# A hybrid attention and recurrence block: sticks times values in plain float32, and four more merge gates in the second stage

## The chip, the cores and the metric

The kernel runs on one core of a Trainium2 chip. The metric is the device time of one execution in microseconds (us); lower is better. PE is the matmul engine (PEld its weight loads), DVE the vector engine, ACT the scalar engine, POOL the general engine, SP the queue that issues most loads. SBUF is the working memory, PSUM the accumulator memory that PE writes to.

## The reference, cut to what matters

A residual block on 1040 rows (16 learned rows ahead of 1024) of width 1024. One projection makes ten streams. Four of them feed stick-breaking attention with 8 heads of 64 channels, four a gated recurrence (HGRN2), and the last two are sigmoid gates, `gate_sb` and `gate_hg`, with which the two branches are merged channel by channel.

```python
proj = u @ w_in[l]
(sb_q, sb_k, sb_v, sb_gate, hg_q, hg_f, hg_i, hg_gate, gate_sb, gate_hg) = jnp.split(proj, bounds, axis=-1)
...
z = jnp.einsum('bhtd,bhsd->bhts', qb, k)
valid = s_idx[None, :] < t_idx[:, None]
log_beta = jax.nn.log_sigmoid(z)
log_1mb = jnp.where(valid, jax.nn.log_sigmoid(-z), 0.0)
later = lax.cumsum(log_1mb, axis=3, reverse=True) - log_1mb
weights = jnp.where(valid, jnp.exp(log_beta + later), 0.0)
return jnp.einsum('bhts,bhsd->bhtd', weights, v)
...
y_sb = (_stick_breaking(sb_q, sb_k, sb_v) * jax.nn.silu(sb_gate)).astype(dtype)
merged = (jax.nn.sigmoid(gate_sb) * (y_sb @ w_sb_out[l]) + jax.nn.sigmoid(gate_hg) * (y_hg @ w_hg_out[l]))
h = h + merged @ w_out[l]
```

The kernel doesn't form the weights themselves. It keeps the running product of `1 - beta` along the keys (the sticks that are left, called sticks here) and multiplies it by differences of neighbouring values, which gives the same sum.

## The kernel before, in words

Channels lie on the partitions and time along the free axis, in tiles of 128 x 128 where blocks are turned. Precision is kept by splitting: a float32 operand is copied to a reduced float32 type (`F32R`, the high part, on ACT) and the rest is subtracted (the low part, on DVE or POOL). A product is then three matmuls, high x high, high x low, low x high (`piece_quanta`, L244 to L263, matmul L259).

**Stages.** First the input is normalised, turned and split (to 68 us). The second stage (L424 to L500, 67.7 to about 267 us) makes those projections that need no order: queries, attention gates, recurrence queries and gates, and six of the sixteen merge-gate groups (`N_GS`, L40). A *twin* there is 256 output channels for all 1024 rows, computed by a scheme of seven products in place of eight (`product`, L458): each product is 12 matmuls of 512 columns (L466). Its weights are split on ACT (L454) and POOL (L455), sums of them are made on DVE (L448 to L451), and the results go to DRAM through the ACT queue. A merge-gate group that is not made there is made later by `gate_group` (L998): 128 channels, two pieces of 512 rows, 24 matmuls each on L259.

**Attention.** A pair of heads has its key and value projections in `pair_groups` (L526). The differences of values are turned to rows by keys (`v_blocks`, L557; `v_meta_block` for the 16 learned rows) and split in two parts side by side, 64 columns of high and 64 of low part for each head. A unit (`Unit`, L593) is one head and two blocks of 128 queries, g = 0 to 3. `scores` makes the scores (L626), sigmoids on ACT (L628) and the running products on DVE (scans, L631 and L635). `values` turns the sticks in banks of two key blocks (`bank_t`, transposes L668), splits each bank into a high part (ACT, L670) and a low part (DVE, L671), and multiplies (`bank_av`, L682): the values are the stationary operand, and the sticks stream past, 256 queries at a time, four matmuls for a bank, one more for the learned rows (L685). Blocks beyond the diagonal are zeros that were set once. The result has the high values' product on partitions 0 to 63 and the low ones' on 64 to 127; ACT copies one half (L688), DVE adds the other (L689) and applies the last difference and the gate (L693), in the layout that the next stage wants.

**Order.** The program is written out in quanta with a cost in ns each. `zip_quanta` lays the scores of the next unit between the values of the current one, and `interleave` (L297) puts *fill* between the quanta of the main work, in proportion to the costs, 4000 ns ahead (`LEAD_A`). Fill of attention is the next pair's key and value projections, the first recurrence head's projection, and merge-gate groups by `FILL` = (2, 1, 1, 1) for the four pairs (L42, L1093 to L1101). Five more groups are fill of the recurrence (L1128). Buffers of one tag rotate; the tag `wt` has two, which the sticks' banks hold in the attention stage and which the recurrence's queries take after it (L774, loaded through SP at L776). PSUM has two banks for turning (`tr`) and one for this accumulator (`av`).

Of the kernel before, what the change touches and what calls it, by code (L numbers as in the profile page):

```python
# [15 lines left out]
P = 128  # L16
# [20 lines left out]
REAL = [(NM, 512), (NM + 512, 512)]  # L37
FULL = [(0, 348), (348, 346), (694, 346)]
QUART = [(0, 256), (256, 256), (512, 256), (768, 272)]
N_GS = 6  # L40
WS = 456
FILL = (2, 1, 1, 1)  # L42


@with_exitstack
def block_kernel(ctx: ExitStack, tc: tile.TileContext, x, meta, norm_g, w_in, w_sb_out,
# [18 lines left out]
    def sb(tag, shape, dt=F32):  # L65
        p = base if tag in HOME else here[-1]
        return p.tile(shape, dt, tag=tag, name=nm(tag), bufs=BUFS.get(tag, 1))
# [358 lines left out]
    twins += [(C_HQ + 2 * P * k, 2 * k, out_silu(kept_hq, HG_SCALE)) for k in range(2)]  # L426
    twins += [(C_HG + 2 * P * k, 2 * k, out_silu(kept_hg, 1.0)) for k in range(2)]
    twins += [(C_GS + 2 * P * k, 2 * k, out_gate(C_GS)) for k in range(N_GS // 2)]

    def ured(c0, t0):  # L430
        return uh[:, c0:c0 + 4, t0:t0 + HT], ul[:, c0:c0 + 4, t0:t0 + HT]
# [73 lines left out]
    here.append(ctx.enter_context(phase("rest")))  # L505


    t = sb("wt", [P, 2, 2, 512], F32R)
    V.memset(t[:, :, :, 0:P].bitcast(F32), 0.0)
    wt_last = [t[:, k] for k in range(2)]  # L510
    t = sb("wt", [P, 2, 2, 512], F32R)
    wt_full = [t[:, k] for k in range(2)]
    n_full = [0]
    t = sb("wtm", [P, 2, 256], F32R)
    V.memset(t.bitcast(F32), 0.0)
    wt_meta = [t[:, k] for k in range(2)]
    t = sb("vm", [P, 2, 2, P], F32R)
    V.memset(t.bitcast(F32), 0.0)
    v_meta = [t[:, k] for k in range(2)]

    later = sb("later", [P, WS])
# [4 lines left out]
    def pair_groups(p):  # L526
        st = {}

        def bk():
            st["k"] = [sb("stk", [P, L], F32R) for _ in range(2)]  # L530
            st["y"] = sb("y", [P, SEQ])
            nc.sync.dma_start(st["y"], kept_sg[p])

        def bv():
            st["vt"] = sb("pt", [P, L + 1])
            st["dv"] = sb("pt", [P, L + 1])
            st["ve"] = sb("ve", [P, NB])
            V.memset(st["vt"][:, 0:1], 0.0)

        def ek(acc, t0, n):  # L540
            for hh in range(2):
                r0, r1 = hh * 64, 64 - hh * 64
                kst = st["k"][hh]
                src = acc[r0:r0 + 64]
                hi = kst[r0:r0 + 64, t0:t0 + n]
                S.activation(hi, src, AF.Copy)
                V.tensor_tensor(kst[r1:r1 + 64, t0:t0 + n], src, hi.bitcast(F32), op=ALU.subtract)

        def ev(acc, t0, n):

            vt = st["vt"]
            S.activation(vt[:, t0 + 1:t0 + n + 1], acc, AF.Copy)
            V.tensor_tensor(st["dv"][:, t0:t0 + n], vt[:, t0:t0 + n], acc, op=ALU.subtract)
            if t0 + n == L:
                G.tensor_copy(st["ve"], vt[:, NM + P:NM + P + (NB - 1) * P + 1:P])

        def v_blocks(b4):  # L557
            def emit():
                if b4 == 0:
                    st["v"] = [sb("v", [P, NB, P], F32R) for _ in range(2)]  # L560
                tp = ps("tr").rearrange("p (b n) -> p b n", b=4)
                for b in range(4):
                    t0 = NM + (b4 * 4 + b) * P
                    T.transpose(tp[:, b], st["dv"][:, t0:t0 + P], ident)
                for hh in range(2):
                    src = tp[:, :, hh * 64:hh * 64 + 64]
                    hi = st["v"][hh][:, b4 * 4:b4 * 4 + 4, 0:64]
                    S.activation(hi, src, AF.Copy)
                    V.tensor_tensor(st["v"][hh][:, b4 * 4:b4 * 4 + 4, 64:128], src, hi.bitcast(F32), op=ALU.subtract)
            return (440.0, emit)  # L570

        def v_meta_block():
            vm = v_meta[p % 2]
            st["vm"] = vm
            tp = ps("tr")
            T.transpose(tp[:NM, 0:P], st["dv"][:, 0:NM], ident)
            for r0 in (0, 32):
                src = tp[:NM, 0:P].rearrange("p (h n) -> p h n", h=2)
                S.activation(vm[r0:r0 + NM, :, 0:64], src, AF.Copy)
                V.tensor_tensor(vm[r0:r0 + NM, :, 64:128], src, vm[0:NM, :, 0:64].bitcast(F32), op=ALU.subtract)  # L580

        after_v = [v_blocks(0), v_blocks(1), (110.0, v_meta_block)]
        return st, [proj(C_V + P * p, FULL, ev, bv, after_v), proj(C_K + P * p, FULL, ek, bk)]

# [8 lines left out]
    class Unit:  # L593
# [46 lines left out]
        def values(self):  # L640

            st, hh, g, k = self.st, self.hh, self.g, self.k
            r0 = hh * 64
            wts = {}
            q = []

            def meta_t():
                tp = ps("tr")
                for qi in range(2):
                    T.transpose(tp[:NM, qi * P:(qi + 1) * P], self.w[qi][:, 0:NM], ident)  # L650
                wm = wt_meta[k]
                with tc.high_priority(offset=HP):
                    S.activation(wm[0:NM], tp[:NM, :256], AF.Copy)
                    V.tensor_tensor(wm[32:32 + NM], tp[:NM, :256], wm[0:NM].bitcast(F32), op=ALU.subtract)

            def bank_t(gg):
                def emit():
                    tp = ps("tr")
                    if gg < g:
                        cols = [(j, qi, (j * 2 + qi) * P) for qi in range(2) for j in range(2)]  # L660
                        wt, lo, where = wt_full[n_full[0] % 2], 0, (0, 256)
                        n_full[0] += 1
                    else:
                        cols = [(0, 0, 2 * P), (1, 1, P), (0, 1, 3 * P)]
                        wt, lo, where = wt_last[k], P, (256, 0)
                    for j, qi, c in cols:
                        s0 = NM + (2 * gg + j) * P
                        T.transpose(tp[:, c:c + P], self.w[qi][:, s0:s0 + P], ident)  # L668
                    with tc.high_priority(offset=HP):
                        S.activation(wt[:, 0, lo:], tp[:, lo:], AF.Copy)  # L670
                        V.tensor_tensor(wt[:, 1, lo:], tp[:, lo:], wt[:, 0, lo:].bitcast(F32), op=ALU.subtract)  # L671
                    wts[gg] = (wt, where)
                return (440.0, emit)

            def bank_av(gg):
                def emit():
                    if gg == g:
                        self.av = ps("av")[:, :256]
                    wt, where = wts[gg]
                    for part in range(2):  # L680
                        for j in range(2):
                            T.matmul(self.av, st["v"][hh][:, 2 * gg + j], wt[:, part, where[j]:where[j] + 256],  # L682
                                     start=(gg == g and part == 0 and j == 0), stop=False)
                    if gg == 0:
                        T.matmul(self.av, st["vm"][:, hh], wt_meta[k], start=False, stop=True)  # L685
                        av = self.av
                        tmp = sb("sg", [P, 256])
                        S.activation(tmp[0:64], av[64:128], AF.Copy)  # L688
                        V.tensor_tensor(tmp[r0:r0 + 64], av[0:64], tmp[0:64], op=ALU.add)  # L689
                        for qi in range(2):  # L690
                            b = 2 * g + qi
                            y = st["y"][r0:r0 + 64, P * b:P * (b + 1)]
                            V.scalar_tensor_tensor(y, tmp[r0:r0 + 64, qi * P:(qi + 1) * P], st["ve"][r0:r0 + 64, b:b + 1], y,  # L693
                                                   op0=ALU.add, op1=ALU.mult)
                return (440.0 + 110.0 * (gg == 0), emit)

            q.append(bank_t(g))
            if g > 0:
                q.append(bank_t(g - 1))
            q.append((220.0, meta_t))  # L700
            for gg in range(g, -1, -1):
                q.append(bank_av(gg))
                if gg > 1:
                    q.append(bank_t(gg - 2))
            return q

    def zip_quanta(a, b):

# [381 lines left out]
    late_q = stream(pairs[1][1][:1], pairs[1][1][1])  # L1090
    emit_all(late_q[:CUT])
    emit_all(zip_quanta(late_q[CUT:], both(units[0], "scores")))
    rest = [gate_group(C_GS, e) for e in range(N_GS, 8)] + [gate_group(C_GH, e) for e in range(8)]  # L1093
    share = FILL
    side, k0 = [], 0
    for p in range(4):
# [6 lines left out]
    for p in range(4):  # L1103
        main = []
        for i in range(6 * p, 6 * p + 6):
            main.append((0.0, lambda i=i: ahead(i + 2)))
            nxt = both(units[i + 1], "scores") if i + 1 < len(units) else []
            main += zip_quanta(both(units[i], "values"), nxt)
            if 7 <= i < 7 + len(MASKS):
                main.append((0.0, lambda h=MASKS[i - 7]: mask_after(h)))  # L1110
        steps.append((main, stream(side[p], side[p + 1][0] if p < 3 else heads[1][1][0])))
# [12 lines left out]
    for h in range(4):  # L1124
        main, t = recurrence(h, heads[h][0], ("q", "ab", "v", "ab")[h])
        main = main[:2] + tail + main[2:]
        tail = t + [hg_gate(h)]
        n = (1,1,2,1)[h]  # L1128
        some, rest = rest[:n], rest[n:]
        if h < 3:  # L1130
            fill = stream(heads[h + 1][1] + some, heads[h + 2][1][0] if h < 2 else (rest + sbg)[0])
# [259 lines left out]
```

## Time and profile before

| what | us |
|---|---|
| median of 3 runs (892.25 to 893.4) | 892.31 |
| the profiled execution | 892.41 |
| its span, first to last instruction | 890.7 |
| PE, PEld busy | 868.2, 750.6 |
| DVE, ACT, POOL busy | 626.2, 410.9, 280.3 |

In a row of grouped instructions stand the line, the engine, the operation, the tiles (result <- operands), the shape and the count, then busy time in us and mean ns of one, then the idle time ahead of them and who ended it. A PE record's end is modelled and neighbours overlap, so distances between starts say more than lengths. In the view by windows stand, for each engine, busy time and number of instructions, and last the granted clock, the share of the DMA engines and GB/s.

### The profile page before, as it was taken

What the parts mean: (1) busy time and instruction counts of PE and PEld (TensorE: products, weight loads), DVE (VectorE), ACT (ScalarE), POOL (GpSimd) and SP (SyncE); (2) the same over time, 40 slices, a digit from 0 to 9 for tenths busy, and PEclk for the clock granted to TensorE, in tenths of its full rate; (3) what the DMA queues carried; (4) which work ended last, traced back from release to release, by engine and by line L of the source; (5) the groups of instructions that cost most, each with busy time, mean ns of one, the idle gap of its engine ahead of it and who ended that gap; (6) DMA issues with size and microseconds to landing.
All of it is one profiled execution on the core that took longest, in us unless ns stands there. A gap on an engine that the chain in (4) does not pass through costs nothing.

```text
span 890.7 us, 15024 instructions
## 1 busy us (share of the span) xinstructions
PE 868.2 (97%) x5684; PEld 750.6 (84%) x5684; DVE 626.2 (70%) x1084; ACT 410.9 (46%) x950; POOL 280.3 (31%) x303
## 2 busy tenths in 40 slices
PE   7999999999999999999999999999999999999996
PEld 5998888888888998899899898879788788888885
DVE  6894455645433378789789788867665989998875
ACT  7763334333432455556556556434435364223432
POOL 1027444544451211123211122447261100004551
PEclk9999999999999999999999999999999999999999
DMA  9223444333343512311213212212312357663212
GB/s 286 67 71 93 160 145 131 95 107 118 119 130 116 169 41 67 96 60 48 84 60 96 86 59 60 84 44 102 121 63 80 129 182 259 197 222 125 95 47 96
DMA packets 90587, 98.12 MB, mean 110 GB/s; under 512 B 6017, under 2 KB 65281, under 8 KB 90514
## 3 DMA queue, kind: packets, MB, share of 16 engines
q1 hardware_dynamic: 76832, 73.78, 27.4%
q10 hardware_dynamic: 13682, 23.37, 7.1%
q8 instruction: 45, 0.74, 0.3%
q14 instruction: 28, 0.23, 0.1%
HBM read 71.94 MB, written 25.20 MB: 109 GB/s over the span
## 4 chain that ended last, share of the span: by engine, by line
PE 84%; DVE 8%; ACT 4%; issue 1%; DMA 1%; POOL 0%; ACTq 0%; SPq 0%; DVEq 0%; POOLq 0%
PE acc L259 33%; PE acc L466 10%; PE z L466 7%; PE tr L466 7%; PE acc L1298 4%; PE av L682 3%; PE tr L668 3%; PE z L626 3%; PE z L1298 3%; PE tr L1298 3%; PE acc L350 2%; DVE ab L635 2%; DVE ab L631 1%; ACT sq L169 1%; PE av L949 1%
## 5 line engine op out<-in xcount | busy, mean ns | idle before, releaser
L259 PE MATMUL acc<-uh,wh 128*128 128x346 f32 (+2 forms) x472 | 173.4, 367 | 0.0
L120 POOL TENSOR_TENSOR wl<-wr,wh 128x256 fp32r<-128x256 f32 x92 | 79.0, 879 | 271.8 <-ACT wh L115 244.2
L259 PE MATMUL acc<-ul,wh 128*128 128x346 f32 (+2 forms) x472 | 164.2, 348 | 0.0
L259 PE MATMUL acc<-uh,wl 128*128 128x346 f32 (+2 forms) x472 | 163.8, 347 | 0.0
L259 PEld LDWEIGHTS acc<-uh,wl 128*128 128x128 f32 x472 | 88.8, 188 | 6.8
L259 PEld LDWEIGHTS acc<-uh,wh 128*128 128x128 f32 x472 | 89.0, 189 | 4.2 <-issue 0.4
L259 PEld LDWEIGHTS acc<-ul,wh 128*128 128x128 f32 x472 | 89.2, 189 | 2.9 <-issue 0.4
L455 POOL TENSOR_TENSOR pw<-su,pw 128x512 fp32r<-128x512 f32 x44 | 59.2, 1365 | 42.8 <-ACT pw L454 42.8
L455 POOL TENSOR_TENSOR pw<-wr,pw 128x512 fp32r<-128x512 f32 x33 | 43.7, 1323 | 62.5 <-ACT pw L454 62.5
L628 ACT ACTIVATE ab<-z 128x456 f32<-128x456 f32 (+6 forms) x112 | 49.8, 448 | 26.4 <-PE z L626 25.9
L631 DVE TENSOR_TENSOR_SCAN ab<-ab,later 128x456 f32<-128x456 f32 (+3 forms) x64 | 55.7, 871 | 6.8 <-ACT ab L628 6.1
L466 PE MATMUL acc<-th,pw 128*128 128x512 f32 x176 | 58.0, 390 | 0.0
L671 DVE TENSOR_TENSOR wt<-tr,wt 128x384 fp32r<-128x384 f32 (+1 forms) x80 | 50.4, 630 | 10.0 <-ACT wt L670 7.8
L670 ACT ACTIVATE wt<-tr 128x384 fp32r<-128x384 f32 (+1 forms) x80 | 44.3, 554 | 26.0 <-PE tr L668 25.8
L682 PE MATMUL av<-wt,v 128*128 128x256 f32 x320 | 52.6, 286 | 3.7 <-DVE sg L689 3.1
L626 PE MATMUL z<-stk,q 128*128 128x456 f32 (+6 forms) x224 | 55.8, 331 | 0.0
L454 ACT ACTIVATE pw<-su 128x512 fp32r<-128x512 f32 x44 | 26.0, 626 | 60.9 <-DVE su L449 27.1
L682 PEld LDWEIGHTS av<-wt,v 128*128 128x128 f32 x320 | 46.2, 188 | 8.3 <-DVE sg L689 5.3
L635 DVE TENSOR_TENSOR_SCAN ab<-ab 128x348 f32<-128x348 f32 (+4 forms) x48 | 47.0, 980 | 7.2 <-ACT ab L628 5.7
L668 PE MATMUL tr<-ident,ab 128*128 128x128 f32 x288 | 45.2, 273 | 0.7 <-DVE ab L631 0.7
L115 ACT ACTIVATE wh<-wr 128x256 fp32r<-128x256 f32 x92 | 34.4, 413 | 24.6 <-PE acc L259 15.6
L626 PEld LDWEIGHTS z<-stk,q 128*128 128x128 f32 x224 | 38.3, 189 | 3.4
(378 smaller groups left out, 2035.4 us busy)
## 6 DMA issues: line engine op xcount, KB each, us to landing
wr<-in_w_in SPq DMA_DIRECT2D x48, 512.0 KB, 4.1
q<-q SPq DMA_DIRECT2D x32, 256.0 KB, 4.2
wr<-in_w_out SPq DMA_DIRECT2D x16, 512.0 KB, 3.5
sg<-gate SPq DMA_DIRECT2D x24, 256.0 KB, 3.2
gate<-sg ACTq DMA_DIRECT2D x20, 256.0 KB, 2.0
xb<-in_x SPq DMA_DIRECT2D x7, 512.0 KB, 8.1
gate<-co ACTq DMA_DIRECT2D x12, 256.0 KB, 2.0
pt<-hi SPq DMA_DIRECT2D x4, 520.0 KB, 3.2
```

Source lines behind the costliest of these rows:

```text
L120: eng.tensor_tensor(lo[:, cs], raw[:, cs], h[:, cs].bitcast(F32), op=ALU.subtract)
L259: T.matmul(acc, a, b, start=(k == 0), stop=(k == total - 1))
L455: G.tensor_tensor(t[:, 1], d[key], t[:, 0].bitcast(F32), op=ALU.subtract)
L466: T.matmul(acc, t[:, part // 2, c], (bh, bl, bh)[part][:, c], start=(c == part == 0), stop=(c == 3 and part == 2))
L626: T.matmul(z, qt[:, k, qo + qi * P:qo + (qi + 1) * P], st["k"][hh][:, c0:c1], start=(k == 0), stop=(k == 1))
L628: S.activation(a[:, c0:c1], z, AF.Sigmoid, scale=-1.0)
L631: ins = V.tensor_tensor_scan(w, w, later[:, WS - (n - c0):][:, ::-1], 1.0, op0=ALU.mult, op1=ALU.max)
L635: V.tensor_tensor_scan(w, w, w, a[:, c1:c1 + 1], op0=ALU.mult, op1=ALU.bypass)
L668: T.transpose(tp[:, c:c + P], self.w[qi][:, s0:s0 + P], ident)
L671: V.tensor_tensor(wt[:, 1, lo:], tp[:, lo:], wt[:, 0, lo:].bitcast(F32), op=ALU.subtract)
L682: T.matmul(self.av, st["v"][hh][:, 2 * gg + j], wt[:, part, where[j]:where[j] + 256], start=(gg == g and part == 0 and j == 0), stop=False)
L1298: T.matmul(a, t[:, part // 2, c], (bh, bl, bh)[part][c][:, n * HT // 2:n * HT // 2 + a.shape[-1]], start=(c == part == 0), stop=(c == 3 an ...
```

## The change

Three things. First, the sticks are no longer split: `bank_t` makes one float32 copy on ACT, `bank_av` multiplies in plain float32, with a 128 x 128 block of sticks as the stationary operand and 64 columns of values streaming, so that the result has queries on the partitions. Blocks beyond the diagonal are left out. Second, the result is copied by ACT into `by_query`, and when both heads of a pair have a unit, `close` turns it back with two transposes and applies difference and gate on all 128 partitions, two quanta into the values of the next unit. Third, the second stage makes four more merge-gate groups (two twins: `N_GS` 8, `N_GH` 2), and `FILL` becomes (0, 0, 0, 1), so that the attention stage has one group as fill. The diff, without the lines that change nothing but spaces:

```diff
-N_GS = 6
+N_GS = 8
+N_GH = 2
 WS = 456
-FILL = (2, 1, 1, 1)
+FILL = (0, 0, 0, 1)
...
     twins += [(C_GS + 2 * P * k, 2 * k, out_gate(C_GS)) for k in range(N_GS // 2)]
+    twins += [(C_GH + 2 * P * k, 2 * k, out_gate(C_GH)) for k in range(N_GH // 2)]
...
-    t = sb("wt", [P, 2, 2, 512], F32R)
-    V.memset(t[:, :, :, 0:P].bitcast(F32), 0.0)
-    wt_last = [t[:, k] for k in range(2)]
-    t = sb("wt", [P, 2, 2, 512], F32R)
-    wt_full = [t[:, k] for k in range(2)]
+    t = sb("wt", [P, 4, 512])
+    wt_full = [t[:, k] for k in range(4)]
     n_full = [0]
-    t = sb("wtm", [P, 2, 256], F32R)
-    V.memset(t.bitcast(F32), 0.0)
+    t = sb("wt", [P, 2, NB, P])
+    by_query = [t[:, k] for k in range(2)]
+    t = sb("wtm", [NM, 2, 256])
     wt_meta = [t[:, k] for k in range(2)]
-    t = sb("vm", [P, 2, 2, P], F32R)
-    V.memset(t.bitcast(F32), 0.0)
+    t = sb("vm", [NM, 2, P])
     v_meta = [t[:, k] for k in range(2)]
...
-                    st["v"] = [sb("v", [P, NB, P], F32R) for _ in range(2)]
+                    st["v"] = sb("v", [P, NB, P])
...
-                for hh in range(2):
-                    src = tp[:, :, hh * 64:hh * 64 + 64]
-                    hi = st["v"][hh][:, b4 * 4:b4 * 4 + 4, 0:64]
-                    S.activation(hi, src, AF.Copy)
-                    V.tensor_tensor(st["v"][hh][:, b4 * 4:b4 * 4 + 4, 64:128], src, hi.bitcast(F32), op=ALU.subtract)
+                S.activation(st["v"][:, b4 * 4:b4 * 4 + 4], tp, AF.Copy)
...
-            for r0 in (0, 32):
-                src = tp[:NM, 0:P].rearrange("p (h n) -> p h n", h=2)
-                S.activation(vm[r0:r0 + NM, :, 0:64], src, AF.Copy)
-                V.tensor_tensor(vm[r0:r0 + NM, :, 64:128], src, vm[0:NM, :, 0:64].bitcast(F32), op=ALU.subtract)
+            S.activation(st["vm"], tp[:NM, 0:P], AF.Copy)
+        st["o"] = by_query[p % 2]
...
-                    S.activation(wm[0:NM], tp[:NM, :256], AF.Copy)
-                    V.tensor_tensor(wm[32:32 + NM], tp[:NM, :256], wm[0:NM].bitcast(F32), op=ALU.subtract)
+                    S.activation(wt_meta[k], tp[:NM, :256], AF.Copy)
...
-                    if gg < g:
-                        cols = [(j, qi, (j * 2 + qi) * P) for qi in range(2) for j in range(2)]
-                        wt, lo, where = wt_full[n_full[0] % 2], 0, (0, 256)
-                        n_full[0] += 1
-                    else:
-                        cols = [(0, 0, 2 * P), (1, 1, P), (0, 1, 3 * P)]
-                        wt, lo, where = wt_last[k], P, (256, 0)
-                    for j, qi, c in cols:
+                    cols = [(0, 0), (0, 1), (1, 1)] + [(1, 0)] * (gg < g)
+                    wt = wt_full[n_full[0] % 4]
+                    n_full[0] += 1
+                    for c, (j, qi) in enumerate(cols):
                         s0 = NM + (2 * gg + j) * P
-                        T.transpose(tp[:, c:c + P], self.w[qi][:, s0:s0 + P], ident)
+                        T.transpose(tp[:, c * P:c * P + P], self.w[qi][:, s0:s0 + P], ident)
+                    n = len(cols) * P
                     with tc.high_priority(offset=HP):
-                        S.activation(wt[:, 0, lo:], tp[:, lo:], AF.Copy)
-                        V.tensor_tensor(wt[:, 1, lo:], tp[:, lo:], wt[:, 0, lo:].bitcast(F32), op=ALU.subtract)
-                    wts[gg] = (wt, where)
+                        S.activation(wt[:, :n], tp[:, :n], AF.Copy)
+                    wts[gg] = (wt, cols)
...
-                        self.av = ps("av")[:, :256]
-                    wt, where = wts[gg]
-                    for part in range(2):
-                        for j in range(2):
-                            T.matmul(self.av, st["v"][hh][:, 2 * gg + j], wt[:, part, where[j]:where[j] + 256],
-                                     start=(gg == g and part == 0 and j == 0), stop=False)
-                    if gg == 0:
-                        T.matmul(self.av, st["vm"][:, hh], wt_meta[k], start=False, stop=True)
-                        av = self.av
-                        tmp = sb("sg", [P, 256])
-                        S.activation(tmp[0:64], av[64:128], AF.Copy)
-                        V.tensor_tensor(tmp[r0:r0 + 64], av[0:64], tmp[0:64], op=ALU.add)
-                        for qi in range(2):
-                            b = 2 * g + qi
-                            y = st["y"][r0:r0 + 64, P * b:P * (b + 1)]
-                            V.scalar_tensor_tensor(y, tmp[r0:r0 + 64, qi * P:(qi + 1) * P], st["ve"][r0:r0 + 64, b:b + 1], y,
-                                                   op0=ALU.add, op1=ALU.mult)
-                return (440.0 + 110.0 * (gg == 0), emit)
+                        self.av = ps("av")[:, :P].rearrange("p (q n) -> p q n", q=2)
+                    wt, cols = wts[gg]
+                    for c, (j, qi) in enumerate(cols):
+                        T.matmul(self.av[:, qi], wt[:, c * P:c * P + P], st["v"][:, 2 * gg + j, r0:r0 + 64],
+                                 start=(gg == g and c == 0), stop=False)
+                    if gg > 0:
+                        return
+                    for qi in range(2):
+                        T.matmul(self.av[:, qi], wt_meta[k][:, qi * P:(qi + 1) * P], st["vm"][:, r0:r0 + 64],
+                                 start=False, stop=(qi == 1))
+                    S.activation(st["o"][:, 2 * g:2 * g + 2, r0:r0 + 64], self.av, AF.Copy)
+                return (440.0 + 220.0 * (gg == 0), emit)
...
+        def close(self):
+            st, g = self.st, self.g
+            def emit():
+                tp = ps("tr")
+                for qi in range(2):
+                    b = 2 * g + qi
+                    T.transpose(tp[:, qi * P:(qi + 1) * P], st["o"][:, b], ident)
+                    y = st["y"][:, P * b:P * (b + 1)]
+                    V.scalar_tensor_tensor(y, tp[:, qi * P:(qi + 1) * P], st["ve"][:, b:b + 1], y, op0=ALU.add, op1=ALU.mult)
+            return [(220.0, emit)] if self.hh else []
...
-    rest = [gate_group(C_GS, e) for e in range(N_GS, 8)] + [gate_group(C_GH, e) for e in range(8)]
+    rest = [gate_group(C_GS, e) for e in range(N_GS, 8)] + [gate_group(C_GH, e) for e in range(N_GH, 8)]
...
-            main += zip_quanta(both(units[i], "values"), nxt)
+            vals = both(units[i], "values")
+            vals[2:2] = both(units[i - 1], "close") if i else []
+            main += zip_quanta(vals, nxt)
+            if i + 1 == len(units):
+                main += both(units[i], "close")
```

More of the change, by code (lines that the diff above doesn't have):

```diff
@@ L564, in emit @@
                     T.transpose(tp[:, b], st["dv"][:, t0:t0 + P], ident)
-                for hh in range(2):
-                    src = tp[:, :, hh * 64:hh * 64 + 64]
-                    hi = st["v"][hh][:, b4 * 4:b4 * 4 + 4, 0:64]
-                    S.activation(hi, src, AF.Copy)
-                    V.tensor_tensor(st["v"][hh][:, b4 * 4:b4 * 4 + 4, 64:128], src, hi.bitcast(F32), op=ALU.subtract)
+                S.activation(st["v"][:, b4 * 4:b4 * 4 + 4], tp, AF.Copy)
             return (440.0, emit)
         def v_meta_block():
-            vm = v_meta[p % 2]
-            st["vm"] = vm
+            st["vm"] = v_meta[p % 2]
             tp = ps("tr")
             T.transpose(tp[:NM, 0:P], st["dv"][:, 0:NM], ident)
-            for r0 in (0, 32):
-                src = tp[:NM, 0:P].rearrange("p (h n) -> p h n", h=2)
-                S.activation(vm[r0:r0 + NM, :, 0:64], src, AF.Copy)
-                V.tensor_tensor(vm[r0:r0 + NM, :, 64:128], src, vm[0:NM, :, 0:64].bitcast(F32), op=ALU.subtract)
+            S.activation(st["vm"], tp[:NM, 0:P], AF.Copy)
+        st["o"] = by_query[p % 2]
         after_v = [v_blocks(0), v_blocks(1), (110.0, v_meta_block)]
@@ L650, in meta_t @@
                     T.transpose(tp[:NM, qi * P:(qi + 1) * P], self.w[qi][:, 0:NM], ident)
-                wm = wt_meta[k]
                 with tc.high_priority(offset=HP):
-                    S.activation(wm[0:NM], tp[:NM, :256], AF.Copy)
-                    V.tensor_tensor(wm[32:32 + NM], tp[:NM, :256], wm[0:NM].bitcast(F32), op=ALU.subtract)
+                    S.activation(wt_meta[k], tp[:NM, :256], AF.Copy)
             def bank_t(gg):
@@ L1127, in block_kernel @@
         tail = t + [hg_gate(h)]
-        n = (1,1,2,1)[h]
+        n = (1, 1, 2, 1)[h]
         some, rest = rest[:n], rest[n:]
```

## The prediction

> **What bounds the kernel now.** I read the page first (shares of the engines, chain that ended last), then the stages as windows, then who waited for whom on PE in the attention stage.
>
> ```profile
> span 890.7 us, 15024 instructions
> ...
> PE 868.2 (97%) x5684; PEld 750.6 (84%) x5684; DVE 626.2 (70%) x1084; ACT 410.9 (46%) x950; POOL 280.3 (31%) x303
> ...
> PE 84%; DVE 8%; ACT 4%; issue 1%; DMA 1%; POOL 0%; ACTq 0%; SPq 0%; DVEq 0%; POOLq 0%
> ```
>
> The two stages that the change touches are the second (67.7 to 267 us, the seven-product projections) and the attention stage (309 to 573 us). In the windows view, each pair is busy time and count, in the order PE, PEld (weight loads), DVE, ACT, POOL:
>
> ```profile
> 67.70:267.00 199.30, 199.30 (x868) 162.79 (x868) 97.41 (x143) 74.76 (x130) 103.28 (x80) 1.00 0.38 122
> 309.00:573.00 264.00, 259.20 (x1706) 237.97 (x1705) 213.37 (x368) 150.43 (x367) 56.48 (x78) 1.00 0.24 71
> ```
>
> PE is busy for all 199.30 us of the second stage and for 259.2 of 264 us of the attention stage, at a granted clock of 1.00. DVE has 213 us of work in the attention stage, but a busy engine is no limit while PE never waits for it. The waits of PE there are these (us in total, times, longest):
>
> ```profile
> PE av L682 <- DVE sg L689: 3.1, 5, 0.9
> PE tr L668 <- DVE ab L631: 0.7, 1, 0.7
> PE tr L792 <- DVE wt L671: 0.5, 1, 0.5
> PE av L682 <- DVE wt L671: 0.3, 1, 0.3
> ```
>
> So both stages run at the pace of PE, and an edit is worth what it takes from or adds to PE's own steps. "Busy" on PE is no price, since records overlap; the price of a matmul is the time from its start to the next start. The timeline of PE in the attention stage gives these steps:
>
> ```profile
> 354.46 0.66 PE L682 MATMUL av<-wt,v 128*128 128x256 f32 x4
> 354.95 0.28 PE L685 MATMUL av<-wtm,vm 128*128 128x256 f32 x1
> 355.06 0.39 PE L259 MATMUL acc<-uh,wl 128*128 128x512 f32 x1
> 355.30 0.93 PE L668 MATMUL tr<-ident,ab 128*128 128x128 f32 x7
> 355.98 0.47 PE L259 MATMUL acc<-uh,wh 128*128 128x512 f32 x1
> 356.29 0.39 PE L259 MATMUL acc<-ul,wh 128*128 128x512 f32 x1
> 356.52 0.40 PE L259 MATMUL acc<-uh,wl 128*128 128x512 f32 x1
> ```
>
> Five sticks-times-values matmuls of 256 columns take 354.46 to 355.06, 0.12 us each. A matmul of 512 columns takes 0.24 (355.06 to 355.30) or 0.23 (356.29 to 356.52), so 0.235. From 355.30 to 356.29 lie seven transposes and one 512: (0.99 - 0.235) / 7 = 0.108 us for a transpose.
>
> **The change, part by part.** *Gates.* Five of the ten direct gate groups run as fill in the attention stage before, one after; the recurrence keeps five. So four groups leave, each 2 pieces of 24 matmuls of 512: 192 x 0.235 = 45.1 us less PE. Two twins come in the second stage, each 7 products of 12 matmuls: 168 at 199.30 / 868 = 0.2296 us, 38.6 us more. With each twin come weight splits, sums, sigmoids and stores on ACT, DVE, POOL and two queues. ACT (75 us), DVE (97) and POOL (103) have about half of that stage free and PE does not wait there, so these cost nothing; were that cover gone, POOL would come first, with 103.28 / 9 = 11.5 us for a twin of some 20 us. Net: -6.5 us.
>
> *Sticks times values, what goes.* 320 matmuls and 32 for the meta rows go: 352 x 0.12 = 42.2 us.
>
> *What comes.* Every 128 x 128 block of sticks becomes a stationary operand, with 64 columns of values streamed past it, in plain float32. A unit g has 4g + 3 blocks, so 3 + 7 + 11 + 15 = 36 for a head, 288 for 8 heads; 2 meta matmuls for each of 32 units make 64. In all 352 plain matmuls, as many as go. What does one cost? The trace has plain float32 matmuls in the recurrence, with 128 columns:
>
> ```profile
> 600.86 0.38 PE L969 MATMUL z<-v,ab 128*128 128x128 f32 x2
> 601.08 0.39 PE L970 MATMUL z<-stk,wt 128*128 128x128 f32 x2
> 601.30 0.39 PE L969 MATMUL z<-v,ab 128*128 128x128 f32 x2
> 601.52 0.39 PE L970 MATMUL z<-stk,wt 128*128 128x128 f32 x2
> 601.75 0.39 PE L969 MATMUL z<-v,ab 128*128 128x128 f32 x2
> 601.97 0.44 PE L949 MATMUL av<-v,v 128*128 128x128 f32 x2
> ```
>
> Each of these rows is a single matmul of the code, in two records, and each record has a weight load of its own. Ten records take 600.86 to 601.97, 0.111 us each, 0.222 a matmul. With 64 columns the streaming halves, the loads don't. Whether the load or the stream sets the 0.111 is the question of this case. The loads' own durations (mean ns last but the idle time) answer it:
>
> ```profile
> L668 PEld LDWEIGHTS tr<-ident,ab 128*128 128x128 f32 x288 | 35.4, 140 | 5.3 <-DVE ab L631 0.9 <-DVE wt L671 0.4
> ...
> L969 PEld LDWEIGHTS z<-v,ab 128*128 128x128 f32 x64 | 10.1, 191 | 0.4
> ...
> L858 PEld LDWEIGHTS z<-wt,stk 128*32 128x32 f32 x512 | 6.3, 110 | 3.5 <-issue 2.9 <-DVE wt L843 0.3
> ...
> L650 PEld LDWEIGHTS tr<-ident,ab 128*16 128x16 f32 x64 | 5.2, 88 | 3.1 <-DVE wt L671 0.6 <-DVE pt L800 0.2
> ```
>
> A plain load of 128 columns lasts 191 ns, one of 32 columns 110: 81 / 96 = 0.84 ns a column, so the part that grows with columns is 128 x 0.84 = 108 ns, the rest a latency that overlaps. For a transpose it is (140 - 88) / 112 = 0.46 ns a column, 59 ns for 128. That this part is a floor under the step shows where the stream is nearly nothing, eight transposes with 128 stationary columns and 16 streamed:
>
> ```profile
> 43.70 0.66 PE L189 MATMUL tr<-ident,xb 16*128 16x16 f32 x8
> ```
>
> ```profile
> L189 PE MATMUL tr<-ident,xb 16*128 16x16 f32 x8 | 0.7, 211 | 0.0
> ```
>
> Their starts are (0.66 - 0.211) / 7 = 0.064 us apart, the 59 ns and a little more, not an eighth of the 0.108 that 128 streamed columns take. So loads follow each other without overlap, and a plain load asks for 108. I price a record of the new matmuls at 0.111: 704 x 0.111 = 78.1 us. The bounds: 0.064 from below (45.1 us, the rival), and above 0.117, the 108 with the transposes' 64 / 59 on it (82.4 us).
>
> The Trainium skill (TensorE: Matmul & The Clock Gate, section LDWEIGHTS) has a rule that speaks against this change: loading time is the number of stationary columns over 1.2 GHz, however few rows or streamed columns there are, an estimate of 107 ns for 128. The trace agrees for plain loads (108) and not for transposes (59). By that rule the sum would be 704 x 0.107 = 75.3 us for the term, 2.8 us less.
>
> *Closing a pair.* 16 calls, 32 transposes of 128 x 128: 32 x 0.108 = 3.5 us. Their first waits for the ACT copy out of PSUM; behind it on PE stand the next transposes and fill. The call comes two quanta into the next unit, so that copy has some 0.8 us (seven transposes) to be done; I take 0, at most 0.3 us x 16 = 5.
>
> *What leaves DVE and ACT.*
>
> ```profile
> L671 DVE TENSOR_TENSOR wt<-tr,wt 128x384 fp32r<-128x384 f32 (+1 forms) x80 | 50.4, 630 | 10.0 <-ACT wt L670 7.8
> ...
> L693 DVE SCALAR_TENSOR_TENSOR y<-sg,ve,y 64x128 f32<-64x128 f32 x64 | 20.1, 353 | 1.0
> ...
> L689 DVE TENSOR_TENSOR sg<-av,sg 64x256 f32<-64x256 f32 x32 | 13.3, 415 | 17.9 <-ACT sg L688 17.6
> L654 DVE TENSOR_TENSOR wtm<-tr,wtm 16x256 fp32r<-16x256 f32 x32 | 13.3, 414 | 2.3 <-ACT wtm L653 1.4
> ```
>
> 97 us of DVE work go; 32 full-height multiply-adds come back, about 11 us at the 353 ns of L693. That is the large number of this change, and it buys only what PE waited for: 3.4 us at L682. Not all of that, since the one bank of the accumulator still waits for a copy on ACT: -2. Against it about +1 for the recurrence's first query load, which now takes the buffer of the sticks that is used to the last bank (571 instead of 569.5 us), with the weight fetches behind it on SP.
>
> **Sum.** -45.1 + 38.6 - 42.2 + 78.1 + 3.5 - 2 + 1 = +31.9 us. The profiled execution took 892.41 us (span 890.7, 1.7 around it), 0.1 over the median of 892.31. So 924.3 us; I say 925. Its own range is 920 to 934: below, a record at the bare 108 ns (-2.1) and the small terms at their best (-2.4); above, a record at 0.117 (+4.3) and the closing wait at 5.
>
> **Rivals.** *The stream sets the price (not slower).* If loads of the new matmuls hide under each other or under the stream, a record costs 0.056 (half of 0.111) to 0.064. Then 39 to 45 us come in place of 78, and the sum is -1.1 to -7.2: 885 to 891, likeliest 887. It decides where a record falls below (45.1 + 42.2 - 38.6 - 3.5 + 1) / 704 = 0.066 us. For it speaks that the new form streams as much as the old; against it the 0.84 ns a column and the 0.064 of the 16-column transposes, which is already a load's price. The Trainium skill (FP8 and Floating Point Precision, section TensorE Precision Notes) counts a true float32 matmul as four passes, with no word of loads; by that alone an estimate is 4 x 64 / 2.4 GHz = 107 ns a matmul, 37.5 us for 352 and 884 us in all. No trace here shows a plain matmul of 64 columns with a full-width load. Chance 0.14.
>
> *Cover runs out (slower still).* The chain within the attention stage goes through the scans on DVE, while PE is kept at work by fill:
>
> ```profile
> by line: PE acc L259 38.9%; PE av L682 11.5%; PE tr L668 10.0%; PE z L626 9.8%; DVE ab L635 6.3%; DVE ab L631 4.7%; PE tr L650 1.9%; issue 1.8%; DVE wt L671 1.6%; DVE stk L547 1.6%; DVE wtm L654 1.4%; ACT ab L628 1.4%; DVE sg L689 1.2%; ACT
> ```
>
> L635 and L631 hold 11% of 264 us, 29 us. The fill is five gate groups (56 us) and six projections of 72 matmuls of 346 columns (69 us at 0.235 x 346 / 512), so the 45 us that leave are a good third of it, and the first pair keeps only one key projection. If a third of the scans' time comes into the open, PE idles 10 us: 935. Against it: sticks times values now keeps PE longer itself, and the copy after each transpose no longer has a subtraction behind it. Chance 0.14.
>
> **How the numbers follow.** The forecast has 0.72. The range 914 to 938 holds it and the cover rival, and leaves out the stream rival. A difference under 0.2% (1.8 us) is one that a measurement of this kernel cannot tell from none. The stream rival is mostly faster, partly within 1.8 us: faster 0.12, same 0.03, slower 0.85.
>
> **What would show it.** In the profile after: 704 records on the sticks-times-values line with starts 0.11 us apart, and weight loads there back to back (right), or 0.06 apart (stream rival). The second stage 38 to 39 us longer at full PE. The attention stage about 264 - 45.1 - 42.2 + 78.1 + 3.5 = 258 us, with DVE near 120 us busy; if it is 265 or more with PE idle before transposes for the scans, cover ran out; if it is near 225, the loads were hidden and the forecast is wrong.

## The result and the profile after

The changed kernel takes 933.05 us (median of 4 runs, 931.39 to 933.92) against 892.41 of the kernel before: 1.0451 times as long, 95% interval 1.0433 to 1.0469, 40.6 us slower. The forecast was 925, with a range of 914 to 938. The four runs lie further apart than those of the kernel before, and the granted clock differs among them: it was 0.998 in those of 931.39 and 932.70, and 0.997 and 0.996 in those of 933.92 (the profiled one) and 933.39. The page of the changed kernel begins so:

```profile
span 932.2 us, 15598 instructions
...
PE 911.3 (98%) x6044; PEld 791.5 (85%) x6044; DVE 542.6 (58%) x903; ACT 411.4 (44%) x938; POOL 280.4 (30%) x301
```

DVE lost 84 us of work (626.2 to 542.6), and PE gained 43 us of busy time. The stages as windows, columns as before the change:

```profile
67.60:305.00 237.40, 237.40 (x1035) 193.80 (x1034) 110.10 (x164) 88.94 (x155) 125.69 (x103) 1.00 0.38 120
348.00:615.00 267.00, 264.31 (x1901) 248.29 (x1899) 121.35 (x174) 137.64 (x335) 31.88 (x42) 0.99 0.19 55
```

In the attention stage DVE's work fell from 213 to 121 us, and the stage isn't shorter for it: PE is busy for 264 of 267 us. For 3.4 us of that stage the granted clock was half:

```profile
387.12:390.53 3.41, 3.41 (x16) 3.12 (x15) 0.00 (x0) 1.43 (x4) 0.00 (x0) 0.50 0.00 0
```

The matmuls that start there, from 387.07 to 391.04, take 3.97 us; the same ones take 2.40 us in the experiment e3 below, at a clock of 1.00. So some 1.6 us of this profiled execution are clock and not kernel. How far each stage moved is read from first starts. The first score matmul and the first matmul of the recurrence, in the kernel before and in the changed one (durations min/median/max in ns, then first and last start in us):

```profile
L626 PE MATMUL z<-stk,q x224: 228/323/456, 309.3 to 562.9; 128*128 128x456 f32 x16, 128*128 128x348 f32 x16, 128*128 128x328 f32 x16, 128*128 128x392 f32 x16
...
L852 PE MATMUL z<-ab,o x32: 378/392/404, 574.3 to 695.1; 128*32 128x256 f32 x32
```

```profile
L618 PE MATMUL z<-stk,q x224: 228/334/621, 347.9 to 600.8; 128*128 128x456 f32 x16, 128*128 128x348 f32 x16, 128*128 128x328 f32 x16, 128*128 128x392 f32 x16
...
L845 PE MATMUL z<-ab,o x32: 379/391/403, 615.4 to 736.6; 128*32 128x256 f32 x32
```

All up to the scores takes 38.6 us more (309.3 to 347.9), as forecast. The attention stage takes 267.5 us in place of 265.0, 2.5 more, where the terms of the forecast that belong to it come to 7.7 less (-45.1 - 42.2 + 78.1 + 3.5 - 2). What comes after is 0.4 longer (932.2 - 615.4 against 890.7 - 574.3), where 1 was forecast. So the miss of this execution, some 10 us with the 1.6 of the clock in it, lies in the attention stage alone. Adding up the distance from each PE start to the next, each counted to the earlier matmul, gives where that stage's time goes (number of records in brackets; the third column is an experiment told below):

| us | before | after | learned rows at 128 |
|---|---|---|---|
| merge gates as fill | 58.9 (240) | 12.4 (48) | 12.3 (48) |
| other fill | 88.0 (505) | 93.3 (504) | 92.5 (504) |
| sticks times values | 40.0 (320) | 62.2 (576) | 59.8 (576) |
| the same, learned rows | 3.9 (32) | 18.7 (128) | 13.6 (128) |
| scores | 37.9 (224) | 41.1 (224) | 40.8 (224) |
| transposes of sticks | 33.4 (352) | 34.2 (352) | 33.5 (352) |
| transposes of values, closing | 3.1 (36) | 5.6 (68) | 5.6 (68) |
| sum | 265.0 | 267.5 | 258.1 |

Sticks times values with the learned rows went from 43.9 to 80.9 us. The forecast had 42.2 to 78.1, and the parts differ: 576 records at 0.108, and 128 at 0.146. The timeline of PE shows why:

```profile
395.41 1.89 PE L667 MATMUL av<-v,wt 128*128 128x64 f32 x16
397.24 0.65 PE L672 MATMUL av<-vm,wtm 16*128 16x64 f32 x4
397.82 0.43 PE L260 MATMUL acc<-uh,wh 128*128 128x348 f32 x1
398.09 0.32 PE L260 MATMUL acc<-ul,wh 128*128 128x348 f32 x1
```

The four records of the learned rows, which use 16 rows of the array, take 0.58 us to the next start, and the step into them is longer too (0.205 us by the median, where equal neighbours have 0.112). The fill matmul after them takes 0.27 us; behind records with 128 rows it takes 0.24, and behind another matmul of the fill 0.16. The kernel before had this in its trace too, in a place that the prediction doesn't use, the recurrence's learned rows:

```profile
598.98 0.48 PE L947 MATMUL av<-pt,v 16*128 16x128 f32 x2
599.39 0.94 PE L949 MATMUL av<-v,v 128*128 128x128 f32 x6
```

Two records with 16 rows take 0.41 us there, not 0.22.

### The profile page after: what moved, and what is told of

Its sections match the earlier page's. It is cut to its first block, busy times and chain, and to the rows that moved or that the text cites. A ratio compares the mean times of both kernels' runs of the same rounds, so it can differ in the third digit from the quotient of the medians.

```text
span 932.2 us, 15598 instructions
## 1 busy us (share of the span) xinstructions
PE 911.3 (98%) x6044; PEld 791.5 (85%) x6044; DVE 542.6 (58%) x903; ACT 411.4 (44%) x938; POOL 280.4 (30%) x301
## 5 line engine op out<-in xcount | busy, mean ns | idle before, releaser
L260 PE MATMUL acc<-uh,wh 128*128 128x346 f32 (+2 forms) x408 | 151.7, 372 | 0.0
L260 PE MATMUL acc<-uh,wl 128*128 128x346 f32 (+2 forms) x408 | 139.2, 341 | 0.0
L260 PE MATMUL acc<-ul,wh 128*128 128x346 f32 (+2 forms) x408 | 138.9, 341 | 0.0
L121 POOL TENSOR_TENSOR wl<-wr,wh 128x256 fp32r<-128x256 f32 x76 | 61.3, 827 | 228.0 <-ACT wh L116 200.4
L260 PEld LDWEIGHTS acc<-uh,wh 128*128 128x128 f32 x408 | 77.1, 189 | 5.9 <-issue 0.8
L667 PEld LDWEIGHTS av<-v,wt 128*128 128x128 f32 x576 | 72.5, 191 | 0.3
L667 PE MATMUL av<-v,wt 128*128 128x64 f32 x576 | 72.7, 268 | 0.0
L620 ACT ACTIVATE ab<-z 128x456 f32<-128x456 f32 (+6 forms) x112 | 50.3, 449 | 33.5 <-PE z L618 32.1
L456 ACT ACTIVATE pw<-su 128x512 fp32r<-128x512 f32 x52 | 30.5, 625 | 71.0 <-DVE su L451 40.1
L657 ACT ACTIVATE wt<-tr 128x384 f32<-128x384 f32 (+1 forms) x80 | 43.8, 556 | 32.6 <-PE tr L654 31.2
L468 PEld LDWEIGHTS acc<-th,pw 128*128 128x128 f32 x208 | 39.0, 188 | 8.5
L468 PE MATMUL acc<-tl,pw 128*128 128x512 f32 x104 | 40.7, 391 | 0.0
```

The lines of the kernel that those rows point to most:

```text
L121: eng.tensor_tensor(lo[:, cs], raw[:, cs], h[:, cs].bitcast(F32), op=ALU.subtract)
L260: T.matmul(acc, a, b, start=(k == 0), stop=(k == total - 1))
L468: T.matmul(acc, t[:, part // 2, c], (bh, bl, bh)[part][:, c], start=(c == part == 0), stop=(c == 3 and part == 2))
L620: S.activation(a[:, c0:c1], z, AF.Sigmoid, scale=-1.0)
L657: S.activation(wt[:, :n], tp[:, :n], AF.Copy)
L667: T.matmul(self.av[:, qi], wt[:, c * P:c * P + P], st["v"][:, 2 * gg + j, r0:r0 + 64], start=(gg == g and c == 0), stop=False)
```

## The experiments

The theory after the result: PE's own steps set the time; a record of the plain form is paced by its weight load; and a load with another number of rows than its neighbours costs extra. The rivals: the streamed columns set the price, or the miss is cover that the fill no longer gives. Each time stands beside runs of the kernel before on the same chip (892.46 to 892.66 us).

**Twice the stream** (e4); the matmuls of the learned rows are changed likewise, and the copy out of PSUM takes the 64 columns of its own head.

```diff
-self.av = ps("av")[:, :P].rearrange("p (q n) -> p q n", q=2)
+self.av = ps("av")[:, :2 * P].rearrange("p (q n) -> p q n", q=2)
-T.matmul(self.av[:, qi], wt[:, c * P:c * P + P], st["v"][:, 2 * gg + j, r0:r0 + 64], ...)
+T.matmul(self.av[:, qi], wt[:, c * P:c * P + P], st["v"][:, 2 * gg + j], ...)
...
```

> The changed kernel, in which each sticks-times-values matmul (and each for the learned rows) streams 128 columns, the values of both heads of the pair, in place of 64; only the 64 of its own head are used. The weight loads are the same 704. Load theory: a record is paced by its load of 128 stationary columns (0.111 us), so twice the stream costs nothing: 933 us, within 3. Stream theory: a record is paced by its columns, so 704 records go from about 0.055 of stream to 0.111 and the time rises by some 39 us, to 970.

Measured: 935.01 us (934.74 to 935.12), 2 us over the changed kernel. A bank of eight records in the changed kernel and in this one, with the start of what follows:

```profile
375.30 1.00 PE L667 MATMUL av<-v,wt 128*128 128x64 f32 x8
376.11 0.41 PE L260 MATMUL acc<-uh,wh 128*128 128x346 f32 x1
```

```profile
375.43 1.05 PE L667 MATMUL av<-v,wt 128*128 128x128 f32 x8
376.24 0.40 PE L260 MATMUL acc<-uh,wh 128*128 128x346 f32 x1
```

0.81 us both times. Between neighbours with equal rows doubling the stream is free, so up to 128 columns the stream doesn't set the step there. At the learned rows it isn't free: the first of their four records has a step of 0.213 us in place of 0.160 (medians), and by the table's count the 704 records take 85.3 us (64.9 + 20.4) in place of 80.9.

**Half the load** (e5), for the learned rows likewise; the accumulator then has 64 partitions, and half of the result stays zero.

```diff
-T.matmul(self.av[:, qi], wt[:, c * P:c * P + P], ...)
+T.matmul(self.av[:, qi], wt[:, c * P:c * P + 64], ...)
...
```

> The changed kernel, in which only the first 64 queries of each block of 128 are loaded as stationary operand for sticks times values (and for the learned rows); the other 64 queries are left out, their results are zeros. Streamed columns stay at 64, the number of matmuls too. Load theory: a load of 64 columns asks for half of 0.108, so the records between equal neighbours fall from 0.112 to 0.06 us: 576 x 0.05 = 29 us less and a part of the learned rows' records, about 900 us, with some of it lost if PE then waits for the scans. Stream theory, or a fixed price of a plain record: the stream is as long as before, nothing changes, 933 us.

Measured: 915.90 us (915.79 to 916.40), 17 us less, where 29 to 33 were expected. The same bank, and the loads (the mean is the last but the idle time):

```profile
374.70 0.68 PE L668 MATMUL av<-v,wt 128*64 128x64 f32 x8
375.31 0.43 PE L260 MATMUL acc<-uh,wh 128*128 128x346 f32 x1
```

```profile
L668 PEld LDWEIGHTS av<-v,wt 128*64 128x64 f32 x576 | 39.2, 137 | 15.3 <-issue 12.9 <-ACT wh L116 0.4 <-ACT stk L546 0.2
```

A load of 64 columns lasts 137 ns in place of 191, and the step between equal neighbours is 58 ns (median) in place of 112. That is the load's price, shown from the other side. But the bank's gain is 0.81 - 0.61 = 0.20 us, not 8 x 0.054: the step into a bank is now 0.246 us after a 346-column matmul that takes 0.158 elsewhere, the first record's own step is 0.107 in place of the 0.058 of the others, and the step out of the bank is 0.152, where the changed kernel has 0.084. Here a load with another number of columns than its neighbours costs extra too.

**Learned rows at 128 rows** (e3).

```diff
-t = sb("wtm", [NM, 2, 256])
+t = sb("wtm", [P, 2, 256])
+V.memset(t, 0.0)
-t = sb("vm", [NM, 2, P])
+t = sb("vm", [P, 2, P])
+V.memset(t, 0.0)
...
```

> The changed kernel, in which the tiles of the 16 learned rows are filled with zeros to 128 rows, so that their 64 matmuls have 128 rows like their neighbours. Theory of row counts: in the changed kernel a step into, between or out of loads with 16 rows takes about 0.2 us where 0.111 was forecast, which makes the 9 us by which the attention stage is longer than forecast; with equal rows the steps fall to 0.112 and the time to about 923 us. Theory of lost cover: those 9 us are PE waiting for scans that fill no longer covers; row counts change nothing, 933 us.

Measured: 924.46 us (924.26 to 925.12), 8.6 us less than the changed kernel. The same place in the timeline:

```profile
394.31 0.61 PE L669 MATMUL av<-v,wt 128*128 128x64 f32 x4
394.76 0.61 PE L674 MATMUL av<-vm,wtm 128*128 128x64 f32 x4
395.18 0.41 PE L260 MATMUL acc<-uh,wh 128*128 128x348 f32 x1
395.42 0.32 PE L260 MATMUL acc<-ul,wh 128*128 128x348 f32 x1
```

The four records take 0.42 us in place of 0.58, and the step into them falls from 0.205 to 0.112. More multiplications, all by zero, and 0.27 us less for each of 32 units (8.6 / 32). In the table's steps the 704 records lose 7.5 us (80.9 to 73.4), and the fill matmuls right behind the learned rows about 0.5; what is left of the 9.4 us between the two attention stages is about what the clock took.

**The same in the kernel before, the other way** (e9). Its learned rows lie in a tile of 128 rows of which 48 hold something.

```diff
-T.matmul(self.av, st["vm"][:, hh], wt_meta[k], start=False, stop=True)
+T.matmul(self.av, st["vm"][:48, hh], wt_meta[k][:48], start=False, stop=True)
```

> The kernel before, in which the matmul of the learned rows reads only the 48 rows that hold something (high part in rows 0 to 15, low part in rows 32 to 47, zeros between) in place of all 128; the result is the same. Theory of row counts, as a property of PE and not of plain float32: a load with another number of rows doesn't overlap its neighbours' work, so the step into each of the 32 matmuls and the step after it grow by 0.09 us or a little more: 32 x 0.2 = 6 us, 898 to 900 us. If the row count costs only where operands are plain float32: 892.5 us, unchanged.

Measured: 901.01 us (900.96 to 901.51), ratio 1.0096 (1.0080 to 1.0113), 8.4 us slower.

```profile
353.36 0.64 PE L682 MATMUL av<-wt,v 128*128 128x256 f32 x4
353.93 0.38 PE L685 MATMUL av<-wtm,vm 48*128 48x256 f32 x1
354.25 0.50 PE L259 MATMUL acc<-uh,wh 128*128 128x512 f32 x1
354.58 0.40 PE L259 MATMUL acc<-ul,wh 128*128 128x512 f32 x1
```

The four matmuls and the step into the fifth take 0.57 us (0.49 with 128 rows, in the rows that the prediction shows), the fifth 0.32 (0.11), the one after it 0.33 (0.24). By these steps it would be 0.38 x 32 = 12 us; the attention stage grew by 8.8, and PE's idle time in it fell from 4.8 us to 2.3, so a part hides in waits that PE had anyway. The operands are reduced float32 here, so the row count isn't a matter of plain float32 alone.

**The two halves of the change** (e1, e2).

```diff
-N_GS = 8
-N_GH = 2
+N_GS = 6
+N_GH = 0
-FILL = (0, 0, 0, 1)
+FILL = (2, 1, 1, 1)
```

> The plain float32 part alone: the merge gates and the fill as in the kernel before (six groups in the second stage, fill 2, 1, 1, 1). Forecast's step: gates cost 6.5 us less in the second stage than as fill, so without them the time is 933 + 6.5 = 939.5 us. Theory of lost cover: with four groups of fill back in the attention stage PE has no waits there, the 9 us come back, and the time is 930 us or less.

Measured: 935.44 us (935.31 to 935.69). The plain form alone costs 42.8 us, and the gates earn 2.4 on top of it, not 6.5: neither theory's number, in between. The 2.4 is small beside the spread of the changed kernel's runs (2.5 us). Between the two profiled executions, without the 1.6 us at half clock, the gates earn 3.0.

> The gates alone: four more merge-gate groups in the second stage and fill (0, 0, 0, 1), with sticks times values as in the kernel before (split, values stationary). If PE stays covered in the attention stage: 892.4 - 6.5 = 886 us, faster than both kernels. Theory of cover: DVE keeps its 213 us there while the stage shrinks to some 220 us of PE work, so PE waits for scans and subtractions; the gain is eaten, 892 to 900 us.

Measured: 904.41 us (903.58 to 905.20), ratio 1.0130 (1.0114 to 1.0145), 11.7 us slower, more than the theory of cover gave. The attention stage there as a window, and PE's waits in it:

```profile
348.00:585.00 237.00, 221.61 (x1517) 202.79 (x1516) 210.23 (x368) 141.83 (x344) 43.35 (x63) 1.00 0.21 62
```

```profile
PE av L684 <- DVE sg L691: 4.0, 6, 0.8
PE tr L652 <- DVE wt L673: 3.6, 8, 0.6
PE av L684 <- DVE wt L673: 3.0, 6, 1.2
PE tr L670 <- DVE wt L673: 1.5, 3, 0.6
```

PE idles 15.4 us, against 4.8 in the kernel before. Further waits don't show as idle, since a record's modelled end covers them: the 224 score matmuls take 45.6 us from start to start, where they took 37.9. The subtractions on DVE (L673) and the addition (L691), for which PE waited 0.8 and 3.1 us in the kernel before, are most of what it waits for once the fill is gone: 8.1 and 4.0 of the 15.4 us.

**Fewer gates moved, in the kernel before** (e7, e8): one twin more, taken from the attention stage's fill (e7, the diff) or from the recurrence's (e8, where `FILL` stays and the recurrence's `n` becomes (1, 0, 1, 1)).

```diff
-N_GS = 6
+N_GS = 8
-FILL = (2, 1, 1, 1)
+FILL = (1, 1, 0, 1)
```

> The kernel before with two more merge-gate groups in the second stage (one twin), taken from the fill of the attention stage: fill (1, 1, 0, 1). The gates alone, moved by four with fill (0, 0, 0, 1), gave 904.4 us where the price of PE's steps was -6.5. If the loss of cover grows with each group: 892.7 - 3.2 + 4 to 9 = 893 to 898 us. If the loss sits in the pairs that have no gate group at all, one group in the first two pairs keeps it small: 890 to 892 us.

> The kernel before with two more merge-gate groups in the second stage (one twin), taken from the fill of the recurrence: (1, 0, 1, 1) groups for its four heads in place of (1, 1, 2, 1), the attention stage's fill as before. If the recurrence has fill to spare: 892.7 - 3.2 = 889.5 us, faster than both kernels. If its fill is cover like that of the attention stage, PE waits for DVE there: 893 us or more.

Measured: e7 896.15 us (ratio 1.0040, 1.0028 to 1.0053), e8 901.55 (1.0101, 1.0087 to 1.0115). Both slower, by little but with the interval clear of 1. In e7 PE idles 9.3 us in the attention stage in place of 4.8; in e8 it idles 11.4 us in the recurrence in place of 3.7, half of it on one line, and the granted clock there is lower (0.98, 1.00 in the kernel before):

```profile
PE z L858 <- DVE wt L843: 5.6, 4, 2.1
```

```profile
594.00:815.00 221.00, 209.59 (x1985) 173.00 (x1978) 180.34 (x361) 87.59 (x234) 53.09 (x46) 0.98 0.41 132
```

The clock is half in two stretches of 3.41 us, an estimate of 3.4 us lost (half their length); all four runs of e8 have 0.994 to 0.996, the kernel before on that chip 0.997 to 0.998. Without that e8 would still be some 6 us slower. So the fill is cover in both stages, from the first twin on; why the clock fell there was not settled.

**The closing transposes** (e6), on top of e3.

```diff
 for qi in range(2):
-    b = 2 * g + qi
-    T.transpose(tp[:, qi * P:(qi + 1) * P], st["o"][:, b], ident)
+    T.transpose(tp[:, qi * P:(qi + 1) * P], st["o"][:, 2 * g + qi], ident)
+for qi in range(2):
+    b = 2 * g + qi
```

> The kernel with the learned rows filled to 128 rows (924.5 us), with one more edit: the two transposes that close a pair are issued ahead of the two multiply-adds that read them, so that the second transpose doesn't write a PSUM bank that DVE is reading. Theory: PE's 2.5 us of idle time before these transposes, and some waits that show only as longer steps, go: 920 to 922 us. Rival: the fill behind the transpose hides the wait anyway: 924.5 us.

Measured: 920.59 us (920.20 to 920.99), 3.9 less than e3. In the changed kernel one such pair of transposes on PE, and DVE at the same time:

```profile
472.88 0.27 PE L695 MATMUL tr<-ident,wt 128*128 128x128 f32 x1
...
474.86 0.33 PE L695 MATMUL tr<-ident,wt 128*128 128x128 f32 x1 [0.61 <-DVE y L697]
```

```profile
473.18 1.25 DVE L623 TENSOR_TENSOR_SCAN ab<-ab,later 128x456 f32<-128x456 f32 x1 [1.18 <-ACT ab L620]
474.46 0.35 DVE L697 SCALAR_TENSOR_TENSOR y<-tr,ve,y 128x128 f32<-128x128 f32 x1
```

The second transpose writes the bank that the first multiply-add reads, so it waits for that, and that stands behind a scan of 1.25 us on DVE. PE idles 0.61 us here. From e3 to e6 its idle time in the attention stage falls from 3.0 us to 0.9, and the steps of the scores and of the transposes of sticks shrink with it (40.8 to 39.8, 33.5 to 31.4).

**The mended plain form without the gates** (e10): e6 with the gates and the fill of e1.

> The plain float32 form with both mends (learned rows at 128 rows, closing transposes together), with the merge gates and the fill as in the kernel before (six groups in the second stage, fill 2, 1, 1, 1). Without mends the four gates earned 2.4 us (935.4 against 933.0) where PE's steps price them at 6.5. If the missing 4 us were waits at the closing transposes, which fill had covered, the mended form earns nearly the whole price: 920.6 + 6 = 926 to 927 us. If they are lost to scores and transposes that wait for ACT and DVE with less fill between, the gates still earn some 2 to 3 us: 923 us.

Measured: 925.49 us (925.10 to 926.70). The gates earn 4.9 us in the mended form, against 2.4 in the form as it was (3.0 without the clock's share). The closing waits are the likely difference: without mends PE's idle time in the attention stage rises from 1.6 us (e1) to 2.7 with the gates moved, with them from 0.7 to 0.9. The 1.6 of the 6.5 that stays lost shows in the steps of the scores (39.1 to 39.8) and of the transposes of sticks (30.5 to 31.4). No version here beats the kernel before.

## Why the prediction was right or wrong

- **What bounds the kernel.** Right: 92 us of DVE work left the attention stage, and the stage got no shorter.
- **Gates in the second stage, +38.6.** Right: 38.6 to the decimal that the trace gives.
- **Gates out of the fill, -45.1.** Right as PE's own steps (58.9 to 12.4, 46.5), but the gates earn 2.4, not 6.5: 4.1 are missing, or 3.5 between the profiles without the clock's share, and they went with the fill's cover. The rival "cover runs out" had the mechanism, at 10 us; it came to less than half in the plain form, which leaves DVE less to do. In the split form it came to 18 (e2). The prediction's check on the second stage, POOL's 103 us by nine twins, has a wrong divisor (the stage has eleven); it enters no sum, and PE didn't wait there.
- **The price of a plain record.** Right in mechanism and size: 112 ns between equal neighbours, 0.111 forecast; the stream doubled leaves it as it was (e4), the load halved halves it (e5). The stream rival is out. The Trainium skill (FP8 and Floating Point Precision, section TensorE Precision Notes) counts four passes for such a matmul; at 64 streamed columns the measured 0.22 us for a matmul is twice the estimate of 107 ns that the prediction works out from the passes alone, and at 128 it agrees with twice that estimate.
- **"704 records at 0.111".** This is the term that was mis-sized. The forecast priced the 128 records of the learned rows like the others; their 16 rows cost 8.6 us more by the runs and 8.0 by the steps, which e3 takes away; e9 brings the like into the kernel before. With equal rows the term is right. The steps of the 704 records in e3 add up to 73.4 us (59.8 + 13.6), and 57 times the matmul of the fill that follows them takes 0.083 us more than its usual step (0.242 in place of 0.159 at 346 columns). These 4.7 us stand in the table as fill, and the split form has no such step (0.159 behind it); together they make the 78.1 of the forecast.
- **Closing, +3.5 and no wait.** The transposes' steps are 2.0 us; the wait was taken as 0 with a bound of 5 for ACT. It came from DVE instead, through the order of two instructions, and was worth 3.9 (e6, on top of e3).
- **The recurrence's first query load, +1.** It cost nothing: what comes after the attention stage takes 316.34 us in the kernel before and 316.35 in e1.

The sum: of the 8.7 us between 924.3 and 933.05, the row count gives +8.6 and the gates' shortfall (lost cover, closing waits and clock) +4.1, and the plain form without both is 4.2 cheaper than forecast (42.8 - 8.6 = 34.2 against 78.1 - 42.2 + 3.5 - 1 = 38.4). Of these 4.2, 1.7 are the old matmuls, whose steps come to 43.9 and not 42.2; 1.2 are PE's idle time, which fell by 3.2 (4.8 to 1.6 in e1) and not by 2; and 1 is the query load. The direction was right for the reason given. That the time lies even in the prediction's own range of 920 to 934 is partly luck: the top of that range stood for a dearer record and a closing wait on ACT, not for the row count and the cover, and two of the errors nearly cancel.

## What to carry to other kernels

On a kernel that runs at PE's pace, price a matmul by the larger of its load and its stream, with a load for each record: narrow streams past full-width plain float32 loads pay for the loads. Give a small matmul among large ones the same number of rows as its neighbours, with zeros if need be, and read in the trace the steps into and out of it; the same may hold for columns. An off-path engine's work is free only while PE has fill to do; price moved fill by what it covered, not by its own steps alone.

## What the runs showed of the hardware

A matmul's load that differs from its neighbours in the number of rows (16 or 48 against 128) or columns (64 against 128) isn't overlapped as usual. At the learned rows of the changed kernel the step into the four records is 0.205 us (0.112 with 128 rows in e3), the first one's own step 0.160 (0.112), the last one's 0.200 (0.084), and that of the fill matmul behind them 0.264 (0.244): 0.28 us for a unit. Two such matmuls in each of 32 units cost 8.6 us (e3), one cost 8.4 (e9). It isn't so for every load: the transposes with 16 stationary columns stand between neighbours with 128 in the kernel before and pay nothing.

```profile
357.53 0.40 PE L259 MATMUL acc<-uh,wl 128*128 128x512 f32 x1
357.76 0.38 PE L650 MATMUL tr<-ident,ab 128*16 128x128 f32 x2
357.90 0.55 PE L626 MATMUL z<-stk,q 128*128 128x328 f32 x2
```

The step into them is the 0.23 us of a 512-column matmul, and the two take 0.14 us. At the learned rows, the load doesn't last longer:

```profile
L667 PEld LDWEIGHTS av<-v,wt 128*128 128x128 f32 x576 | 72.5, 191 | 0.3
...
L672 PEld LDWEIGHTS av<-vm,wtm 16*128 16x128 f32 x128 | 16.5, 185 | 2.1
```

The Trainium skill (TensorE: Matmul & The Clock Gate, section LDWEIGHTS) says that a load's time depends on its columns and not on its rows. These rows agree, 185 and 191 ns; that the neighbours pay is a thing that only the steps show. Why the overlap is lost was not settled: the runs show that it is, for rows in plain and in reduced float32, for columns in plain float32.

The granted clock can fall to half without idle time ahead of it: in the changed kernel it fell at 387.12, and from 350 to 387 PE was busy for 36.94 of 37 us by the profile. What set it off stays open.
